# Two-layer encoder on one core: earlier weight requests, a pair normed in the tail, one copy fewer per position half, gathers in another buffer ring

## The chip, the cores and the metric

One core of one Trainium2 chip runs the whole program. TensorE (PE) multiplies, VectorE (DVE) and ScalarE (ACT) work element by element, GpSimd (POOL) does some element-wise work and issues some DMAs, SyncE (SP) issues most DMAs. The metric is the device time of one execution in microseconds (us); the time before is the median of three runs. The stages below come from one further execution that was profiled.

## What is computed

Two sequences (2048 and 512 tokens, width 1024) pass through the same trunk, in fp32:

```python
def trunk(x):
    h = rmsnorm(x, attn_norm)                     # layer 0: windowed attention
    z = h @ attn_w_in                             # q (16 heads x 64), k, v (4 heads), gate
    p = exp(q k^T / 8 + bias[key - query]) over |key - query| <= 128, with a sink in the denominator
    x = x + ((p v) * silu(gate)) @ attn_w_out
    h = rmsnorm(x, fourier_norm)                  # layer 1: Fourier mixing
    f = Re(2-D DFT of h over positions and the 256 channels of each of 4 groups)
    x = x + (f * silu(h @ fourier_w_gate)) @ fourier_w_out
    return rmsnorm(x, final_norm)
```

## The kernel before, in words

Each fp32 operand of a large product is split into a high part (rounded, ACT copy) and a low part (the difference, DVE or POOL), and a product is three matmuls (`matmul3`, L91). Tile pools hand out buffers by tag, each tag a ring of a fixed number of buffers: `x` (`xtile`, 4), `hT` (`htile`, 8), `xr` (3), `w` (4), `uT` (8), and in the second layer `L` (`left`, 20) and `R` (`right`, 16). An instruction that fills a new tile waits until all users of the tile that held the buffer are done. Every engine runs its own queue in order; the order within each queue is planned when the program is built, near the order of the code, with explicit edges added by `after` and `seq` (L127, L132) where one instruction must stand behind another.

**Layer 0** goes through five chunks of 512 tokens (`CHUNKS`, L35; chunk 0 is the short sequence). For a chunk, `make_h` loads the transposed x and splits it, `kv_proj` makes k and v, and a loop of 17 steps (L829) runs the attention of eight head pairs: pair p is scored in steps 2p and 2p+1. In step n `at[n // 2 + 1].start()` (L833) requests the bias tile b of a later pair (L426), and in odd steps `loads[n // 2 + 2]()` (L835) brings the next q and gate weights. In chunk 0 a weight comes raw from DRAM (`load_w`, L96: staging tile w32, L110), is split by ACT (L113) and POOL (L118), and its split form is stored for the later chunks; the staging tile is a `uT` buffer, but for pairs 6 and 7, for two `late` weights and for the output weights it is an `xtile` buffer (L109). The xs tiles, from which the sums of squares of the next chunk are made (`stats`, L150; load L169, square L161), take `xtile` buffers too. The splits of softmax rows (`pts`, L521 on ACT and L522 on DVE) feed the product `av` (L539) with v. What is left of the output projection of the last chunk when its loop ends is the *tail*: two empty steps, eight steps of products for the second half of the columns, and the residual add and store (L620, L621).

**Layer 1** first runs the tail while it splits the gate weights (`take`, L1131) and norms the two x tiles of pair 0 (`norms`, L969: a square on ACT L947, a power on POOL L88, a scaling on DVE L972). Then ten pairs of 128-token tiles go through `gates` (L1070): seven products W, X, Z by a Winograd scheme of 2x2 blocks, with hooks between them that turn the next pair (transposes L980, sums, splits) and make its channel transform z. Gates go to DRAM (s2d, L1087). For each of the positions of the transform, `position` (L1274) multiplies with a table of cosines and sines into an even part a and an odd part b, copies a twice on ACT (L1299 into asb of the `xr` ring, L1303 into the result u), forms the two mirrored results on DVE (L1304, L1305), and multiplies by the gate rows s2 (L1307), which `gated` (L1248) reads on SP, or for a mirrored position gathers by row numbers through POOL (L1256). The output projection follows, first `finish` (L1325), for the last eight positions `Outs` (L1338), where the first product's hook `split_g` (L1619) requests the next position's gate rows, and `reads` (L1605) its go tiles. Places: `xtile` is also the place of the x rows for the residual.

Of the kernel before, what the change touches and what calls it, by code (L numbers as in the profile page):

```python
# [9 lines left out]
F32 = mybir.dt.float32  # L10
# [4 lines left out]
ALU = mybir.AluOpType  # L15
# [4 lines left out]
P = 128  # L20
D = 1024
# [21 lines left out]
def encoder(  # L43
# [52 lines left out]
    def load_w(c, n, name, lo_engine=None, late=None):  # L96
# [12 lines left out]
        w32 = stage[late is not None or n > 19 or n in (6, 7, 18, 19)](f"w32{name}")  # L109
        load = SP.dma_start(w32, w_in[n] if n < 20 else w_out[(n - 20) // 4, (n - 20) % 4])  # L110
        if late:
            after(load, late)
# [12 lines left out]
    stage, res_tile, ready, chain = [], [], {}, {}  # L125
# [15 lines left out]
    def attention_phase():  # L141

        with ExitStack() as es:
# [230 lines left out]
            def qg_proj(c, p, hs, res, invb=None):  # L374
# [3 lines left out]

                def load():
                    st["q"] = load_w(c, p, f"q{c}_{p}", None if p else DVE)  # L380
                    st["g"] = load_w(c, 12 + p, f"g{c}_{p}", None if p else DVE)
# [34 lines left out]
                return load, steps  # L416

            def attention(c, p, res, uTs):
# [5 lines left out]
                def start():  # L424
                    bt = ap.tile([P, 2, 386], F32, tag="bias", bufs=2, name=f"b{c}_{p}")
                    SP.dma_start(  # L426
                        bt[:, :, 1:385],
                        bass.AP(rowd.tensor, rowd.offset + p * 1024, [[1, P], [512, 2], [1, 384]]),
                    )
                    st["bias"] = bt  # L430
# [340 lines left out]
            for c in range(len(CHUNKS)):  # L771
# [15 lines left out]
                loads, work = [], []  # L787
                for p in range(8):
                    load, steps = qg_proj(c, p, hs, res[p], invb0)
                    loads.append(load)  # L790
                    work += steps
# [37 lines left out]
                for n in range(17):  # L829
                    new = (at[n // 2], 2 * (n % 2)) if n < 16 else None  # L830
                    old = (at[(n - 1) // 2], 2 * ((n - 1) % 2)) if n else None
                    if n % 2 == 0 and n < 14:
                        at[n // 2 + 1].start()  # L833
# [64 lines left out]
    def fourier_phase(tail):  # L898
        with ExitStack() as es:
# [170 lines left out]
            def gates(pr, hooks):  # L1070
# [53 lines left out]
                hook(5)  # L1124
                prod(W, A[1, 1], wg["N4"], four, False)
# [36 lines left out]
            pairs[0].x = [ready["x", i] for i in range(2)]  # L1162
            ACT.dma_start(gb, bass.AP(g1.tensor, g1.offset, [[0, P], [1, D]]))
            split_steps = [("T", k) for k in range(4)] + [("B", k) for k in (3, 0, 1, 2)]
            for i, s in enumerate(tail):
                s()
                if i in (3, 5):
                    pairs[0].norms((5 - i) // 2)
                if 1 <= i < 9:
# [57 lines left out]
            for n, pr in enumerate(pairs[:-1]):  # L1227
                nx = pairs[n + 1]
                for i in range(2):
                    nx.load(1 - i)  # L1230
                    nx.norms(1 - i)
# [42 lines left out]
            def position(name, tab, gr, gs, tiles, loads=None, parts=None, between=None):  # L1274
# [4 lines left out]
                asb = main.tile([P, 4, P], F32, tag="xr", bufs=3, name=f"as{name}")  # L1279
                us = [zt(f"u{name}_{i}") for i in range(len(tiles))]  # L1280
                for hf in range(2):
# [16 lines left out]
                    sa = asb[:, 2 * hf : 2 * hf + 2]  # L1298
                    ACT.copy(sa, a[:, :, 0:P])  # L1299
                    for i, u in enumerate(us):  # L1300
# [441 lines left out]
```

## Time and profile before

| | |
|---|---|
| median of 3 runs | 1607.68 us (1607.36 to 1610.32) |
| the profiled execution | 1608.39 us |
| its span, first to last instruction | 1606.6 us |
| mean granted TensorE clock | 0.998 of full speed |
| DMA traffic | 373.88 MB, mean 233 GB/s |
| layer 0, up to the end of the tail's products | about 1077 us |

How to read the profile: a *wait* is idle time of an engine, put down to the instruction that ended it. A timeline row gives start, duration, engine, source line, operation, out<-in, and in brackets the idle time before it with its releaser. A window row gives, for a stretch of the span, its length, the busy time of each engine with the number of instructions, the granted clock, the share of DMA engines that were busy, and GB/s. A group row gives the line, engine, operation, shapes and count, then total busy us, mean ns of one, and idle time before. SPq is the sequencer of SyncE, which issues DMAs. PE spans of matmuls are modelled at their end, so neighbours overlap a little.

### The profile page before, as it was taken

The page shows a single profiled execution, that of the slowest core. Times are in us where ns is not written, and L with a number is a line of the kernel's source. Part 1 is how long each engine was busy: PE and PEld are TensorE (multiplying, and loading weights), DVE is VectorE, ACT ScalarE, POOL GpSimd, SP SyncE. Part 2 cuts the span into 40 slices and gives each one's busy share as a digit, 9 for nine tenths or more (in the row PEclk, how much of TensorE's full clock was granted, in tenths as well). Part 3 has the DMA queues.
Part 4 walks back from the last instruction along what each step waited for, and adds up shares of the span by engine and source line. Part 5 has one row for each costly group of instructions (what it writes and reads, how often), then busy time and mean ns, then how long its engine had stood idle before and what let it go on. Part 6 is the DMA issues. An engine that isn't in the chain of part 4 may idle for free.

```text
span 1606.6 us, 27437 instructions
## 1 busy us (share of the span) xinstructions
PE 1587.6 (99%) x9743; PEld 1320.4 (82%) x9743; DVE 1145.6 (71%) x2785; ACT 881.7 (55%) x2112; POOL 446.0 (28%) x613
## 2 busy tenths in 40 slices
PE   9999999999999999999999999999999999999998
PEld 7887888888888888988788888887888887888876
DVE  6787665777547786377764577658878777889786
ACT  6777634676236684257752476636655554343342
POOL 2466651421404314024222242123112111101100
PEclk9999999999999999999999999999999999999999
DMA  7577695656865567655649556665656569458652
GB/s 295 199 289 278 237 349 213 224 220 210 293 218 204 212 238 252 237 207 214 246 157 334 210 207 221 239 223 197 222 210 237 186 219 402 163 196 306 256 198 92
DMA packets 100579, 373.88 MB, mean 233 GB/s; under 512 B 12139, under 2 KB 22379, under 8 KB 83036
## 3 DMA queue, kind: packets, MB, share of 16 engines
q1 hardware_dynamic: 81708, 297.91, 51.9%
q0 software_dynamic: 16400, 70.04, 11.4%
q10 hardware_dynamic: 2336, 4.20, 0.7%
q8 instruction: 77, 1.26, 0.3%
q14 instruction: 58, 0.48, 0.1%
HBM read 280.84 MB, written 91.26 MB: 232 GB/s over the span
## 4 chain that ended last, share of the span: by engine, by line
PE 84%; DVE 4%; issue 4%; DMA 4%; POOL 2%; ACT 2%; POOLq 0%; SPq 0%; DVEq 0%; ACTq 0%
PE gp L94 13%; PE qp L94 13%; PE op L94 9%; PE spt L94 8%; PE spt L455 6%; PE av L539 6%; PE W L94 5%; PE fo L94 4%; PE vp L94 4%; PE pt L513 3%; PE Wo L94 3%; PE Z L94 2%; DMA w32q<-in_w_in_dram 1%; PE z L94 1%; PE Zo L94 1%
## 5 line engine op out<-in xcount | busy, mean ns | idle before, releaser
L474 DVE CUSTOM_DVE_ANT_0 S<-spt,b 128x385 f32<-128x385 f32 (+1 forms) x315 | 154.1, 527 | 128.4 <-PE spt L455 80.2
L94 PE MATMUL gp<-h,wg 128*128 128x512 f32 x960 | 238.6, 397 | 0.0
L94 PE MATMUL qp<-h,wq 128*128 128x512 f32 x960 | 237.1, 396 | 0.0
L521 ACT CAST pts<-pt 128x384 fp32r<-128x384 f32 (+1 forms) x320 | 123.8, 473 | 176.6 <-PE pt L513 176.5
L94 PEld LDWEIGHTS gp<-h,wg 128*128 128x128 f32 x960 | 175.9, 189 | 43.7 <-issue 9.7
L94 PEld LDWEIGHTS qp<-h,wq 128*128 128x128 f32 x960 | 174.9, 188 | 41.3 <-issue 5.5
L482 ACT ACTIVATE S<-S 128x385 f32<-128x385 f32 (+1 forms) x320 | 190.3, 606 | 20.7 <-DVE S L474 18.0
L522 DVE TENSOR_TENSOR pts<-pt,pts 128x384 fp32r<-128x384 f32 (+1 forms) x320 | 147.5, 522 | 28.3 <-ACT pts L521 28.2
L94 PE MATMUL op<-wo,uT 128*128 128x512 f32 x600 | 140.4, 391 | 0.0
L455 PE MATMUL spt<-kwin,qab 64*128 64x384 f32 (+1 forms) x945 | 132.6, 358 | 0.0
L94 PEld LDWEIGHTS op<-wo,uT 128*128 128x128 f32 x600 | 111.9, 188 | 23.9 <-issue 0.7
L563 POOL TENSOR_TENSOR uT<-o,uT 128x256 fp32r<-128x256 f32 x75 | 55.5, 740 | 249.2 <-ACT uT L562 249.1
L539 PEld LDWEIGHTS av<-pts,v 128*128 128x128 f32 x576 | 101.5, 189 | 22.8 <-ACT pts L521 2.8
L539 PE MATMUL av<-pts,v 128*128 128x512 f32 (+1 forms) x576 | 117.2, 343 | 2.4 <-ACT pts L521 1.8
L94 PE MATMUL fo<-wo,tTu 128*128 128x512 f32 x480 | 116.7, 392 | 0.0
L455 PEld LDWEIGHTS spt<-kwin,qab 64*128 64x128 f32 x945 | 85.9, 185 | 31.2 <-issue 24.7
L94 PEld LDWEIGHTS fo<-wo,tTu 128*128 128x128 f32 x480 | 88.5, 188 | 16.7
L494 DVE TENSOR_SCALAR S<-S 128x384 f32<-128x384 f32 (+1 forms) x192 | 90.4, 471 | 6.4
L559 POOL TENSOR_TENSOR o<-o,s 128x256 f32<-128x256 f32 x75 | 55.2, 736 | 134.7 <-DVE o L557 134.4
L94 PE MATMUL spt<-wo,uT 128*128 128x512 f32 x360 | 86.7, 392 | 0.0
L94 PEld LDWEIGHTS spt<-wo,uT 128*128 128x128 f32 x360 | 66.5, 188 | 13.7
L513 PEld LDWEIGHTS pt<-ident,S 64*128 64x128 f32 x1792 | 68.2, 138 | 4.2 <-issue 2.3
(317 smaller groups left out, 3039.4 us busy)
## 6 DMA issues: line engine op xcount, KB each, us to landing
wo<-wsd SPq DMA_DIRECT2D x32, 1024.0 KB, 6.0
wq<-wsd SPq DMA_DIRECT2D x31, 1024.0 KB, 7.4
wg<-wsd SPq DMA_DIRECT2D x31, 1024.0 KB, 5.0
x<-x1d SPq DMA_DIRECT2D x40, 512.0 KB, 4.1
b<-b21d SPq DMA_DIRECT2D x40, 512.0 KB, 5.8
b<-rowd SPq DMA_DIRECT2D x40, 384.0 KB, 4.3
xs<-in_x_dram SPq DMA_DIRECT2D x23, 512.0 KB, 6.7
s2d<-gt POOLq DMA_DIRECT2D x40, 256.0 KB, 3.3
```

The costliest lines, as they stand in the source:

```text
L94: pe(PE.matmul(out, a[i], b[j], start=start and i + j == 0, stop=stop and i == 1, skip_group_check=more))
L455: pe(PE.matmul(banks[j][:, 2 + k0 * P : 2 + k1 * P], res["q"][rows, qp, b * P : (b + 1) * P], kwin[g][rows, kp, b * P + k0 * P : b * P + k ...
L474: seq(DVE, DVE.tensor_tensor_reduce(out=s[:, e0:e1], in0=ps[:, 1 + e0 : 1 + e1], in1=st["bias"][:, j, 386 - e1 : 386 - e0][:, ::-1], scale ...
L482: last_exp[0] = seq(ACT, ACT.activation(s[:, e0:e1], s[:, e0:e1], AF.Exp, bias=s[:, 386:387], scale=-1.0, accum_out=s[:, 387:388]))
L494: seq(DVE, DVE.tensor_scalar(s[:, ks], s[:, ks], den, None, ALU.mult))
L513: pe(PE.transpose(ps[h][:, kb, j, :], ss[j][rows, 1 + kb * P : 1 + (kb + 1) * P], ident[rows, rows]))
L521: seq(ACT, ACT.copy(hi, ps[:, k0:k1]))
L522: seq(DVE, DVE.tensor_tensor(lo, ps[:, k0:k1], f32(hi), ALU.subtract))
L539: pe(PE.matmul(to, v, pt, start=n == part == 0, stop=part == 1 and n in (1, len(todo) - 1), skip_group_check=n > 1,))
L559: eng.tensor_tensor(o, o, s, ALU.mult)
L563: low = eng.tensor_tensor(lo, o, f32(hi), ALU.subtract)
```

## The change

Five edits in one:

1. `fetch_w` is split off `load_w`. In chunk 0 the raw weights of pairs 6 and 7 are requested at the start of steps 8 and 10 (before: in steps 9 and 11), and the bias request of that step is put behind them.
2. The x tiles of pair 1 of the Fourier layer are loaded in the tail (after steps 4 and 5, into `htile` buffers) and normed there (after steps 8 and 10), no longer at the start of pair 0's gates.
3. For the last pair of `gates`, hook 5 stands in the middle of the N4 product instead of ahead of it.
4. `position` copies a once, into the first result; the second result takes only its two edge columns from ACT, and DVE forms all else from the first result, whose real part is overwritten last.
5. `split_g` puts the second tile of gate rows, the gathered one, into `left` always; before it was `xtile` in all but the first round.

```diff
--- before.py
+++ after.py
@@ -93,7 +93,16 @@
         for i, j in ((0, 0), (0, 1), (1, 0)):
             pe(PE.matmul(out, a[i], b[j], start=start and i + j == 0, stop=stop and i == 1, skip_group_check=more))
 
-    def load_w(c, n, name, lo_engine=None, late=None):
+    def fetch_w(n, name, late=None):
+
+        w32 = stage[late is not None or n > 19 or n in (6, 7, 18, 19)](f"w32{name}")
+        load = SP.dma_start(w32, w_in[n] if n < 20 else w_out[(n - 20) // 4, (n - 20) % 4])
+        if late:
+            after(load, late)
+        last_fetch[0] = load
+        return w32
+
+    def load_w(c, n, name, lo_engine=None, late=None, w32=None):
 
         w = wp.tile([P, 2, D], F32R, align_bytes=LINE, tag="w", bufs=4, name=f"w{name}")
         if c == 1 and n in AGAIN:
@@ -106,10 +115,8 @@
         if c:
             SP.dma_start(f32(w), f32(wsd[n]))
             return w[:, 0], w[:, 1]
-        w32 = stage[late is not None or n > 19 or n in (6, 7, 18, 19)](f"w32{name}")
-        load = SP.dma_start(w32, w_in[n] if n < 20 else w_out[(n - 20) // 4, (n - 20) % 4])
-        if late:
-            after(load, late)
+        if w32 is None:
+            w32 = fetch_w(n, name, late)
         ACT.copy(w[:, 0], w32)
         if lo_engine is None:
 
@@ -122,7 +129,7 @@
             (SP if lo_engine else POOL).dma_start(f32(wsd[n]), f32(w))
         return w[:, 0], w[:, 1]
 
-    stage, res_tile, ready, chain = [], [], {}, {}
+    stage, res_tile, ready, chain, last_fetch = [], [], {}, {}, [None]
 
     def after(ins, anchor):
 
@@ -376,9 +383,13 @@
                 steps = []
                 st = {}
 
+                def fetch():
+                    for which, n in (("q", p), ("g", 12 + p)):
+                        st["w32" + which] = fetch_w(n, f"{which}{c}_{p}")
+
                 def load():
-                    st["q"] = load_w(c, p, f"q{c}_{p}", None if p else DVE)
-                    st["g"] = load_w(c, 12 + p, f"g{c}_{p}", None if p else DVE)
+                    for which, n in (("q", p), ("g", 12 + p)):
+                        st[which] = load_w(c, n, f"{which}{c}_{p}", None if p else DVE, w32=st.get("w32" + which))
 
                 def mm(which, k):
                     if k == 0:
@@ -413,7 +424,7 @@
 
                 for which, evac in (("q", evac_q), ("g", evac_g)):
                     steps += [lambda which=which, evac=evac, k=k: one(which, evac, k) for k in range(KD)]
-                return load, steps
+                return fetch, load, steps
 
             def attention(c, p, res, uTs):
 
@@ -421,12 +432,13 @@
                 g = p // 2
                 st = {}
 
-                def start():
+                def start(behind=None):
                     bt = ap.tile([P, 2, 386], F32, tag="bias", bufs=2, name=f"b{c}_{p}")
-                    SP.dma_start(
+                    load = SP.dma_start(
                         bt[:, :, 1:385],
                         bass.AP(rowd.tensor, rowd.offset + p * 1024, [[1, P], [512, 2], [1, 384]]),
                     )
+                    after(load, behind)
                     st["bias"] = bt
                     uT = wp.tile([P, 2, CH], F32R, align_bytes=LINE, tag="uT", bufs=8, name=f"uT{c}_{p}")
                     uTs.append((uT[:, 0], uT[:, 1]))
@@ -784,9 +796,10 @@
                 uTs = []
                 res = [{} for p in range(8)]
                 at = [Heads(*attention(c, p, res[p], uTs)) for p in range(8)]
-                loads, work = [], []
+                fetches, loads, work = [], [], []
                 for p in range(8):
-                    load, steps = qg_proj(c, p, hs, res[p], invb0)
+                    fetch, load, steps = qg_proj(c, p, hs, res[p], invb0)
+                    fetches.append(fetch)
                     loads.append(load)
                     work += steps
                 loads[0]()
@@ -829,8 +842,13 @@
                 for n in range(17):
                     new = (at[n // 2], 2 * (n % 2)) if n < 16 else None
                     old = (at[(n - 1) // 2], 2 * ((n - 1) % 2)) if n else None
+                    behind = None
+                    if c == 0 and n in (8, 10):
+
+                        fetches[n // 2 + 2]()
+                        behind = last_fetch[0]
                     if n % 2 == 0 and n < 14:
-                        at[n // 2 + 1].start()
+                        at[n // 2 + 1].start(behind)
                     if n % 2 and n // 2 + 2 < 8:
                         loads[n // 2 + 2]()
                     chain.setdefault(PE, None)
@@ -1121,8 +1139,12 @@
                 x_step(3)
                 DVE.tensor_tensor(c11, c11, X, ALU.add)
                 silu(c11, 0, 0)
-                hook(5)
-                prod(W, A[1, 1], wg["N4"], four, False)
+                if pr is not pairs[-1]:
+                    hook(5)
+                prod(W, A[1, 1], wg["N4"], (0, 1), False)
+                if pr is pairs[-1]:
+                    hook(5)
+                prod(W, A[1, 1], wg["N4"], (2, 3), False)
                 silu(W, 1, 0)
                 hook(6)
 
@@ -1160,12 +1182,22 @@
             order = [[16, 17, 18, 19]] + [[a, a + 4, a + 8, a + 12] for a in range(4)]
             pairs = [Pair(2 * gi + i // 2, tiles[i : i + 2]) for gi, tiles in enumerate(order) for i in (0, 2)]
             pairs[0].x = [ready["x", i] for i in range(2)]
+
+            def second(i):
+
+                t = pairs[1].x[i] = htile([P, D], F32, f"x1_{pairs[1].ts[i]}")
+                SP.dma_start(t, x1d[pairs[1].ts[i] * P : (pairs[1].ts[i] + 1) * P, :])
+
             ACT.dma_start(gb, bass.AP(g1.tensor, g1.offset, [[0, P], [1, D]]))
             split_steps = [("T", k) for k in range(4)] + [("B", k) for k in (3, 0, 1, 2)]
             for i, s in enumerate(tail):
                 s()
                 if i in (3, 5):
                     pairs[0].norms((5 - i) // 2)
+                if i in (4, 5):
+                    second((4, 5).index(i) ^ 1)
+                if i in (8, 10):
+                    pairs[1].norms((8, 10).index(i) ^ 1)
                 if 1 <= i < 9:
                     w, k = split_steps[i - 1]
                     take(ready[w, k], k, left, *{"T": ("T2", "T1"), "B": ("B11", "B22")}[w])
@@ -1226,9 +1258,10 @@
                 build(k)
             for n, pr in enumerate(pairs[:-1]):
                 nx = pairs[n + 1]
-                for i in range(2):
-                    nx.load(1 - i)
-                    nx.norms(1 - i)
+                if n:
+                    for i in range(2):
+                        nx.load(1 - i)
+                        nx.norms(1 - i)
                 gates(pr, {
                     1: [lambda: turns1(nx)], 2: [lambda: turns2(nx)], 3: [lambda: turns3(nx)], 4: [lambda: turns4(nx)],
                     5: [lambda: nx.z_odd_even()],
@@ -1276,7 +1309,6 @@
                 s2s, tb = loads or position_loads(name, tab, tiles)
                 cs, sn, ns = [(tb[:, 2 * i], tb[:, 2 * i + 1]) for i in range(3)]
                 bp = bank(f"B{name}")
-                asb = main.tile([P, 4, P], F32, tag="xr", bufs=3, name=f"as{name}")
                 us = [zt(f"u{name}_{i}") for i in range(len(tiles))]
                 for hf in range(2):
                     ts = parts[hf] if parts else halves_of(name, gr, gs, hf)
@@ -1295,14 +1327,15 @@
                     acc(a, (cs, ns), 0, 130)
                     b = bp[:, hf * 256 : hf * 256 + 256].rearrange("p (g c) -> p g c", g=2)
                     acc(b, (sn, cs), P, P)
-                    sa = asb[:, 2 * hf : 2 * hf + 2]
-                    ACT.copy(sa, a[:, :, 0:P])
-                    for i, u in enumerate(us):
-                        uv = u.rearrange("p (g c) -> p g c", g=4)[:, 2 * hf : 2 * hf + 2]
-                        ops = (ALU.subtract, ALU.add) if i == 0 else (ALU.add, ALU.subtract)
-                        ACT.copy(uv[:, :, 0 : P + 1], a[:, :, 0 : P + 1])
-                        DVE.tensor_tensor(uv[:, :, 1:P], sa[:, :, 1:P], b[:, :, 1:P], ops[0])
-                        DVE.tensor_tensor(uv[:, :, P + 1 : 256], sa[:, :, 1:P], b[:, :, 1:P], ops[1])
+                    uv = [u.rearrange("p (g c) -> p g c", g=4)[:, 2 * hf : 2 * hf + 2] for u in us]
+                    ACT.copy(uv[0][:, :, 0 : P + 1], a[:, :, 0 : P + 1])
+                    re, im = uv[0][:, :, 1:P], b[:, :, 1:P]
+                    for v in uv[1:]:
+                        ACT.copy(v[:, :, 0 : P + 1 : P], a[:, :, 0 : P + 1 : P])
+                        DVE.tensor_tensor(v[:, :, 1:P], re, im, ALU.add)
+                        DVE.tensor_tensor(v[:, :, P + 1 : 256], re, im, ALU.subtract)
+                    DVE.tensor_tensor(uv[0][:, :, P + 1 : 256], re, im, ALU.add)
+                    DVE.tensor_tensor(re, re, im, ALU.subtract)
                 for u, s2 in zip(us, s2s):
                     DVE.tensor_tensor(u, u, s2, ALU.mult)
                 return list(zip(us, tiles))
@@ -1618,8 +1651,7 @@
 
                 def split_g():
 
-                    places = (xtile, xtile if ft["N4"] else left)
-                    nxt["s"] = [gated(name, r, place) for r, place in zip(tiles, places)]
+                    nxt["s"] = [gated(name, r, place) for r, place in zip(tiles, (xtile, left))]
                     nxt["p"] = [halves_of(name, *gl, hf) for hf in range(2)]
                     if not ft["T3"]:
                         f_sums("T3", right)
```

## The prediction

> **What bounds the kernel now.** I read the page first, then who TensorE waited for, then the stages around the longest waits, cut with the window view.
>
> ```profile
> span 1606.6 us, 27437 instructions
> PE 1587.6 (99%) x9743; PEld 1320.4 (82%) x9743; DVE 1145.6 (71%) x2785; ACT 881.7 (55%) x2112; POOL 446.0 (28%) x613
> ...
> PE av L539 <- ACT pts L521: 1.8, 1, 1.8
> PE tr L1350 <- DVE up L1307: 1.6, 2, 0.8
> ...
> PE trb L980 <- DVE x L972: 1.0, 1, 1.0
> PE W L94 <- ACT c L1097: 1.0, 1, 1.0
> ```
>
> TensorE is busy for 1587.6 of 1606.6 us, and the change removes no matmul. So what can be won is the 19.0 us of its idle time, and whatever slower clock follows an idle stretch. The longest waits lie in four places, and each edit touches one. The sum below is made against the profiled execution: 1608.39 us, 1.79 us more than its span, and 0.71 above the median 1607.68.
>
> **Part 1, weights of pairs 6 and 7 (chunk 0).** The windows below are steps 9, 11 and 13 of the 17-step loop (columns: us; busy us of PE, PEld, DVE, ACT, POOL; clock; DMA share; GB/s), then two cuts of step 11.
>
> ```profile
> 117.43:126.70 9.27, 9.09 (x64) 7.09 (x63) 6.30 (x25) 7.96 (x20) 7.01 (x11) 1.00 0.38 133
> 135.60:148.44 12.84, 10.99 (x65) 8.28 (x64) 8.49 (x29) 9.49 (x22) 8.23 (x12) 0.87 0.60 223
> 148.44:157.23 8.79, 8.79 (x63) 7.10 (x62) 7.45 (x26) 6.50 (x18) 7.58 (x11) 1.00 1.00 376
> ...
> 140.00:142.38 2.38, 0.63 (x3) 0.19 (x1) 1.24 (x4) 2.38 (x6) 2.35 (x4) 1.00 0.02 9
> ...
> 144.20:146.20 2.00, 2.00 (x7) 1.61 (x7) 1.88 (x11) 2.00 (x6) 2.00 (x4) 0.50 0.87 252
> ```
>
> Steps 9 and 11 split the weights of pairs 6 and 7. A step without a stall takes 8.79 us; step 9 took 9.27 and step 11 took 12.84, so 0.48 and 4.05 us too much. Only 1.8 us of that is idle TensorE; the rest is the clock, 0.50 in the two microseconds after it. The chain behind it, from the timeline, with one line of the chain of work (DMA w32q, 12.41 us to landing):
>
> ```profile
> 119.81 2.84 POOL L118 TENSOR_TENSOR wq<-w32q,wq 128x256 fp32r<-128x256 f32 x4 [1.48 <-ACT wq L113]
> ...
> 123.54 0.38 SPq L426 DMA_DIRECT2D b<-rowd  x1
> 124.01 1.80 SPq L169 DMA_DIRECT2D xs<-in_x_dram  x2
> 126.42 0.33 SPq L110 DMA_DIRECT2D w32q<-in_w_in_dram  x1
> ...
> 126.42 12.41 DMA w32q<-in_w_in_dram
> ...
> 138.91 1.05 ACT L113 CAST wq<-w32q 128x1024 fp32r<-128x1024 f32 x1 [3.59 <-DMA w32q<-in_w_in_dram]
> ...
> 144.97 1.04 ACT L161 ACTIVATE xs<-xs 128x1024 f32<-128x1024 f32 x1
> ...
> 147.39 0.19 ACT L437 COPY b<-sk 128x4 f32<-128x4 f32 x1
> ```
>
> SP's queue is in order. Pair 7's q is requested at 126.42, behind bias b (held until its buffer frees) and two xs loads; ACT, free at 138.91 - 3.59 = 135.32, waits for it, and the casts of pts that TensorE's av needs are queued behind on ACT. The edit puts both requests ahead of b. They still need a staging buffer of the xtile ring (4). One that is sure: pair 6's q leaves its buffer when POOL ends, at 119.81 + 2.84 = 122.65. Plus 12.41 that lands at 135.06, just before ACT is free; DMA engines are only 38% busy in step 9, so 12.41 is an upper price. Pair 6 is requested earlier in the same way. I take 4.3 of 0.48 + 4.05 = 4.53; bounds 0 and 4.5. What it costs: b, and the chunk-1 xs loads, come behind two more requests (0.33 us as the q row, g's alike) and their buffers, g's at worst 126.4, so b is 2.9 us later than 123.54; its first user on ACT is at 147.39, some 20 us on. Next late after the stall: nothing near, as step 13 shows, with no idle time at the same ACT load.
>
> [...]
>
> **Part 2, pair 1 of the Fourier layer normed in the tail.** Stage of pair 0's gates, then a later pair's for comparison; then the queues.
>
> ```profile
> 1081.87:1114.98 33.11, 30.44 (x165) 24.80 (x162) 28.40 (x47) 23.99 (x48) 11.20 (x14) 1.00 0.53 190
> ...
> 1140.35:1166.02 25.67, 25.67 (x141) 22.22 (x141) 18.73 (x31) 15.19 (x29) 4.92 (x9) 1.00 0.55 195
> ...
> 1074.98 2.05 DVE L620 TENSOR_TENSOR xr<-xr,op 128x512 f32<-128x512 f32 x3 [4.38 <-PE op L94]
> 1075.96 1.90 POOL L621 DMA_DIRECT2D x1d<-xr  x3 [10.89 <-DVE xr L620]
> ...
> 1077.46 1.07 ACT L987 CAST tTb<-trb 128x512 fp32r<-128x512 f32 x2 [16.72 <-PE trb L980]
> ...
> 1088.25 0.32 SPq L967 DMA_DIRECT2D x<-x1d  x1
> ...
> 1089.85 1.09 ACT L947 ACTIVATE jkb<-x 128x1024 bf16<-128x1024 f32 x1
> ...
> 1092.50 1.76 DVE L972 SCALAR_TENSOR_TENSOR x<-x,invb,g1b 128x1024 f32<-128x1024 f32 x1 [0.74 <-POOL invb L88]
> ```
>
> The first stage takes 7.44 us more. It has 24 more matmuls; at 25.67/141 = 0.18 us each that is 4.4, so 3.0 are waits. Now x is asked for at 1088.25 for want of an xtile buffer, squared on ACT at 1089.85 and scaled on DVE at 1092.50; TensorE waits 1.0 for that and 1.0 for an ACT copy queued among these squares. Moved: per tile one SP load, one square (1.09 on ACT), one one-column power on POOL, a short and a long DVE operation (up to 1.76). Their new cover is the idle time in the last three brackets: 16.72 on ACT, 10.89 on POOL, 4.38 on DVE, for 2.2 us of squares, two powers, and at most 3.8 on DVE. Without that cover the DVE part would stand before the residual adds and cost up to 3.8. On SP the loads pass the last wo loads, which do wait for buffers; a stuck load there would hold them. The x tiles now take two of eight hT buffers, those of split gate weights. Next late is DVE: 28.40 of 33.11 busy, still some 25 of 30. So not all comes back: I take 2.6 of 3.0; bounds -3.8 and 3.0.
>
> **Part 3, hook order and no copy of real parts.** The first row, from the chain of work, is for the time of one product (chunk 1's k).
>
> ```profile
> 221.88 10.88 PE spt L94 x48
> ...
> 1340.02 1.98 PE L932 MATMUL tru<-ident,us 128*128 128x128 f32 x14 [0.50 <-DVE us L1307]
> ...
> 1349.71 0.37 ACT L1299 COPY ass<-As 128x256 f32<-128x256 f32 x1 [1.72 <-DMA s2d<-gt]
> ...
> 1350.41 0.39 PE L94 MATMUL As<-gs,tbs 128*128 128x260 f32 x1 [0.65 <-ACT us L1303]
> ...
> L1303 ACT COPY up<-Ap 128x258 f32<-128x258 f32 x32 | 10.8, 391 | 0.9 <-DVE gp L1270 0.9
> ...
> L1304 DVE TENSOR_TENSOR up<-asp,Bp 128x254 f32<-128x254 f32 x32 | 13.2, 414 | 6.0 <-PE Bp L94 4.5 <-ACT up L1303 1.3
> L1299 ACT COPY asp<-Ap 128x256 f32<-128x256 f32 x18 | 6.7, 374 | 25.0 <-PE Ap L94 15.5 <-DVE gp L1270 9.2
> ```
>
> The transposes at 1340.02 wait 0.50 for DVE; with six N4 products put ahead of them (10.88/48 = 0.23 each, 1.4 us), that wait is covered. The hook's one w_fout load on SP goes 1.4 us later too; I count that at nothing, 1.4 at most. The dropped copy (asb) also held a buffer of the xr ring, and ACT stood 1.72 us at 1349.71 for a gate store that had not landed; that goes, and with it the 0.65 that TensorE waited next. Also gone: 24 copies of 0.37 (18 asp, 6 ass), and 16 of 0.39 shrink to four elements a row, not shown at this place (between 0 and 0.39; 0.19 as the b<-sk row, the nearest). That is 24 x 0.37 + 16 x 0.20 = 12.1 us off ACT, which idles elsewhere there (25.0 us ahead of L1299), so I count it at nothing. DVE keeps its operations (0.41 each); one a half now works in place, which may cost nothing or as much as a second 0.41. I take nothing, since the scaling of x in part 2 works in place too; at 0.41 the two halves that TensorE awaits here lose 0.8. Sum: 0.50 + 0.65 and the small waits right behind them: 1.3; bounds -0.8 and 2.
>
> **Part 4, mirrored gathers in the left ring.**
>
> ```profile
> 1502.06:1527.04 24.98, 24.13 (x126) 20.20 (x125) 21.15 (x37) 10.61 (x22) 3.25 (x5) 1.00 0.53 194
> 1527.04:1553.26 26.22, 24.99 (x126) 20.31 (x124) 22.55 (x40) 12.26 (x25) 2.47 (x3) 1.00 0.60 204
> 1553.26:1577.21 23.95, 23.95 (x125) 20.41 (x124) 21.29 (x37) 11.25 (x23) 2.45 (x3) 1.00 0.48 164
> ...
> 1518.65 1.01 POOL L1256 DMA_INDIRECT s2p<-s2d,mir  x1 [4.73 <-DVE up L1305]
> ...
> 1543.32 1.01 POOL L1256 DMA_INDIRECT s2p<-s2d,mir  x1 [4.79 <-DMA out_dram<-x]
> ```
>
> Three rounds of the same products take 24.98, 26.22 and 23.95 us: 1.03 + 2.27 = 3.3 over the last. In the first two the gather is issued late, waiting for an xtile buffer (in the second, for an output store to land), and TensorE then waits 1.6 for DVE's product with it. In left, 16 of 20 buffers hold w_out and N4; four are free for F (two), a table and this tile, so it need not wait. The xtile buffer it leaves lets the x loads on SP go earlier, and the go loads behind them. I take 2.3; bounds 0 and 3.3.
>
> **Sum.** 4.3 + 2.6 + 1.3 + 2.3 = 10.5: 1608.39 - 10.5 = 1597.9; against the median 1597.2. I forecast **1597.5**. By their upper bounds the parts give 12.8 to 14 together with the small waits near them: 1594.
>
> **Rivals.**
>
> ```profile
> 221.96 1.28 DVE L211 SCALAR_TENSOR_TENSOR h<-xk,g0s,h 128x512 fp32r<-128x512 f32 x1 [3.87 <-ACT h L210]
> ```
>
> - *Pair 7 is still late*: the ring gives its buffer only at about 126.4. Part 1 shrinks to 0.5: 1601.7. For it: four buffers for four weights and five xs tiles. Against: 122.65 is enough.
> - *Given back in chunk 1*: its h tiles come from a DMA and POOL chain that does not move. Against: the seventh h is done at 221.96 + 1.28 = 223.24 and wanted at 221.88 + 6/8 x 10.88 = 230.0 (its products are the row of 48), 6.8 us later. If so, 1608.39 - 6.2 = 1602.2.
> - *DVE takes over in the Fourier layer* (86% busy in pair 0's stage and in the slow round): only part 1 comes, 1604.1.
> - *Idle time alone comes back*: the clock falls for another reason; part 1 gives 1.8 + 0.5, so 1599.9. [...]
> - *Not what it says*: the order that is planned at compile time keeps the requests and norms where they were: 1607.7.
> - *Slower*: pair 7's request gets the buffer of the last xs tile, whose square ends at 144.97 + 1.04 = 146.0. With 12.41 it lands at 158.4, 19.6 us after 138.83; ACT, and so TensorE, stand that much longer: 1608.4 - 6.2 + 19.6 = 1622. It passes the old time once the request goes out later than 126.4 + 6.2 = 132.6. Against: two buffers come free before.
>
> **How the numbers follow.** Forecast 0.50; pair 7 still late 0.15; chunk 1 0.05; DVE 0.13; idle alone 0.04; nothing 0.05; slower 0.08. A measurement tells 0.2% (3.2 us) from no change, so faster is below 1604.5, slower above 1610.9. Faster: 0.50 + 0.15 + 0.05 + 0.04 and half of the DVE case, 0.80; within: its other half and nothing, 0.12; slower 0.08. The range, 1593.5 to 1604.5, takes in all but the last two and half of the DVE case.
>
> **What would show it.** Part 1: w32q for pair 7 issued before b and by 123, no ACT wait at its cast, step 11 near 8.8 with clock 1.00. Part 2: pair 1's squares before the transposes of pair 0; the stage near 30.5. Part 3: no wait ahead of tru and As. Part 4: gathers about 10 us earlier, rounds near 24. I am wrong if step 11 still shows a wait for w32q, if b is late, or if new DVE waits of a microsecond stand in the Fourier stages.

## The result and the profile after

| | before | after |
|---|---|---|
| median, beside each other on one chip | 1607.52 us (6 runs, 1605.77 to 1610.32) | 1595.33 us (6 runs, 1594.02 to 1596.69) |
| the profiled execution | 1608.39 us | 1594.57 us |
| TensorE idle | 19.0 us | 11.2 us |

The ratio is 0.9924, with a 95% interval from 0.9911 to 0.9936: 12.2 us faster by the medians, 13.8 by the two profiled executions. Forecast were 1597.5 us, and 10.5 us off. Line numbers behind L95 are higher in the kernel after: the product av is now at L551, ACT's casts of pts at L533, the add to c at L1136, the gather at L1289.

First the page after, span and busy time, then all that TensorE waited for over 0.2 us (total, times, longest).

```profile
span 1592.8 us, 27377 instructions
...
PE 1581.6 (99%) x9743; PEld 1319.4 (83%) x9743; DVE 1145.4 (72%) x2785; ACT 871.7 (55%) x2088; POOL 447.5 (28%) x613
```

```profile
PE idle L239 <- DVE idle L236: 1.2, 1, 1.2
PE W L94 <- DVE c L1136: 1.0, 1, 1.0
PE Bp L94 <- DVE up L1338: 0.3, 1, 0.3
PE Ap L94 <- DVE gp L1303: 0.3, 1, 0.3
```

Every wait that the prediction quoted from before is gone, and one of 1.0 us is new (W for DVE's c). Of the 13.8 us, 7.8 are idle time; the other 6.0 are a shorter busy time of the same 9743 matmuls. Now the stages, cut at the same matmuls as before: steps 9, 11 and 12 of chunk 0, pair 0's stage, and two of the last rounds. (The prediction calls its third window step 13; it begins where step 11 ends, so it is step 12.)

```profile
117.29:126.11 8.82, 8.82 (x64) 7.16 (x63) 7.59 (x28) 8.14 (x22) 2.54 (x4) 1.00 0.99 377
...
134.22:143.08 8.86, 8.86 (x65) 7.21 (x64) 7.83 (x29) 8.17 (x21) 6.04 (x9) 1.00 0.69 226
143.08:151.86 8.78, 8.78 (x63) 7.09 (x62) 7.83 (x27) 6.89 (x18) 6.40 (x10) 1.00 0.89 318
...
1070.38:1107.68 37.30, 36.81 (x212) 31.43 (x211) 31.05 (x51) 25.90 (x52) 11.26 (x16) 1.00 0.56 206
1508.26:1532.22 23.96, 23.96 (x125) 20.32 (x124) 21.15 (x37) 10.07 (x21) 4.06 (x4) 1.00 0.60 192
1532.22:1556.16 23.94, 23.94 (x126) 20.32 (x124) 21.17 (x37) 10.16 (x21) 3.45 (x3) 1.00 0.59 193
```

Read the first two numbers of a row: where they agree, TensorE never stood. Step 9 is 8.82 (9.27 before), step 11 is 8.86 (12.84), at clock 1.00. Pair 0's stage, here cut from its first transpose to the next pair's first Z, is 37.30 us long (1076.83 to 1117.27 before: 40.44). The rounds are even at 23.95.

The whole difference, by the starts of the same matmuls in the two profiles:

| from | to | before | after | gained |
|---|---|---|---|---|
| start | first product of chunk 1 | 221.71 | 216.30 | 5.41 |
| there | first transpose of pair 0 | 855.12 | 854.08 | 1.04 |
| there | first Z of pair 1 | 40.44 | 37.30 | 3.14 |
| there | last X of the last pair | 221.41 | 220.52 | 0.89 |
| there | transposes of the second position | 48.96 | 47.72 | 1.24 |
| there | first Xo | 107.15 | 107.58 | -0.43 |
| there | last Xo | 96.04 | 93.50 | 2.54 |

The rows add up to 13.83. The 1.04 belongs to no part: item 4 alone, whose code there is that of before, takes 853.94 for the same stretch. The last row differs between executions too: seven profiles have the rounds of before, and take 96.04 to 97.91 us from first to last Xo; that of the kernel before is the shortest of them.

### The profile page after: what moved, and what is told of

It reads as the page before. It is cut to its first block, busy times and chain, and to the rows that moved or that the text cites. A ratio compares the mean times of both kernels' runs of the same rounds, so it can differ in the third digit from the quotient of the medians.

```text
span 1592.8 us, 27377 instructions
## 1 busy us (share of the span) xinstructions
PE 1581.6 (99%) x9743; PEld 1319.4 (83%) x9743; DVE 1145.4 (72%) x2785; ACT 871.7 (55%) x2088; POOL 447.5 (28%) x613
## 5 line engine op out<-in xcount | busy, mean ns | idle before, releaser
L533 ACT CAST pts<-pt 128x384 fp32r<-128x384 f32 (+1 forms) x320 | 123.5, 473 | 176.2 <-PE pt L525 176.1
L551 PEld LDWEIGHTS av<-pts,v 128*128 128x128 f32 x576 | 101.4, 188 | 18.7
L551 PE MATMUL av<-pts,v 128*128 128x512 f32 (+1 forms) x576 | 115.7, 341 | 0.0
```

What stands on the lines that cost most here:

```text
L533: seq(ACT, ACT.copy(hi, ps[:, k0:k1]))
L551: pe(PE.matmul(to, v, pt, start=n == part == 0, stop=part == 1 and n in (1, len(todo) - 1), skip_group_check=n > 1,))
```

## The experiments

Twelve kernels. Each median stands beside runs of the kernel before on the same chip (its median in brackets). To begin with, each part alone on the kernel before.

### The parts alone

Part 1 (diff item 1) alone:

> The kernel before with the early weight requests alone. Theory (each part removes its own wait, and the parts add): step 11 falls from 12.84 to about 8.9 us and steps 9 and 10 by 0.5 together to 1.3, so 5.2 us less by the two profiles, 1602.4; the Fourier stages stay as before, with the waits of 1.0 for x and for c in pair 0's gates. Rival (what the chunk loop wins, a later DMA-bound stage takes back): step 11 is short, but chunk 1 or the tail begins less than 3 us earlier, 1605 or more. Rival (the clock falls for another reason than the wait): the clock of 0.5 stays somewhere in steps 9 to 13, 1605.

Measured: 1602.56 us (1608.11), ratio 0.9965 [0.9953, 0.9978], 5.55 us off.

Part 2 (item 2) alone:

> The kernel before with pair 1's load and norm in the tail alone. Theory: pair 0's gate stage gets 3 to 4 us shorter, because ACT and DVE lose two squares and two scalings there, 1604.0; nothing else changes. Rival (it only moves the wait: DVE is 86% busy in that stage and the next one): the waits for x and c go, others of the same total come, less than 1.5 us, 1606.5. Rival (the tail pays): TensorE idles between the tail's last product and the first transposes by more than a microsecond.

Measured: 1604.6 us (1608.11), ratio 0.9977 [0.9968, 0.9987], 3.5 us off. Pair 0's stage is 37.19 us.

Of part 3, item 4 alone, so without the hook edit:

> The kernel before without the copy of real parts, with the hook where it was. Theory (the gain of part 3 is the copy's alone, since in the changed kernel a wait of 1.0 for DVE's add of c stands where the hook's wait of 0.5 was): the wait of 0.65 ahead of the As products goes, together with ACT's 1.72 for the gate store, and the wait of 0.5 for the turned tile stays: 1.3 to 1.6 us less, 1606.2. Rival (the hook's move gave it): less than 0.5 us, 1607.2.

Measured: 1606.35 us (1608.11), ratio 0.9989 [0.998, 0.9999], 1.8 us off. TensorE's timeline after the last X of the last pair is that of the kernel after, though the hook stands where it stood before:

```profile
1336.71 0.84 PE L94 MATMUL X<-b,tTb 128*128 128x512 f32 x3
1338.57 1.69 PE L94 MATMUL W<-wN,tTb 128*128 128x512 f32 x6 [1.01 <-DVE c L1118]
1340.09 1.04 PE L932 MATMUL tru<-ident,us 128*128 128x128 f32 x8
```

Six N4 products (W<-wN) now run ahead of the transposes (tru), and they wait 1.01 us, where the theory kept the wait of 0.50 for the turned tile.

Part 4 (item 5) alone:

> The kernel before with the gathered gate rows in the left ring alone. Theory: the second and third gather are issued some 10 us earlier, the two waits of 0.8 for DVE's product with them go, the rounds come to about 24 us: 2.5 us less, 1605.2. Rival (the gain came from the ACT copies that part 3 removes in the same rounds): the gathers are early, but the rounds keep more than half of the 3.3 us, 1606.5.

Measured: 1605.03 us (1608.11), ratio 0.9981 [0.9971, 0.999], 3.1 us off.

The four add up to 13.9 us, and together they give 12.2: nothing shows that one part takes much from another.

**What the same code shows five times.** Layer 0 is the same in the kernels before, part 2 alone, item 4 alone, part 4 alone and the load of part 2 alone (below). Still its step 11 waited 1.75, 1.16, 1.66, 0.51 and 0.46 us, and steps 9 to 12 took 39.80, 38.63, 38.55, 37.26 and 37.35 us, against 34.57 after. So part 1 is worth 5.2, 4.1, 4.0, 2.7 or 2.8 us by these steps, according to the execution; the profile on which the prediction rests held the largest. The wait goes with one transfer: pair 7's q, requested 9.2 us ahead of step 11 each time, took 12.4, 11.8, 12.3, 11.1 and 11.1 us to land.

### Which of the two requests?

Part 1 alone with the early request of only one pair:

```diff
-                    if c == 0 and n in (8, 10):
+                    if c == 0 and n == 8:
```

> The kernel before, with the early request for pair 6 alone (at step 8); pair 7's weights are asked for as before, behind bias b and the xs tiles. My theory: the stall of step 11 is pair 7's q, requested at 126.4 and 12.4 us on its way. Then only step 9's 0.5 us comes back, step 11 still waits 0.5 to 1.8 us for the casts of pts, and the time is 1607.3 (1606.5 to 1608). Rival, the delay begins with pair 6 and is handed on (pair 6's late split holds the staging buffers of pair 7): most of part 1 comes, 1604 or less, and step 11 is near 8.9 us.

Measured: 1603.26 us (1607.12), ratio 0.9978 [0.9968, 0.9987], 3.9 us off. Its steps 9 and 11, and SP's queue between them:

```profile
117.01:125.83 8.82, 8.82 (x63) 7.16 (x62) 7.59 (x28) 7.46 (x21) 2.54 (x4) 1.00 0.67 223
...
133.94:142.80 8.86, 8.86 (x63) 7.21 (x63) 8.18 (x28) 8.54 (x22) 7.43 (x12) 1.00 0.50 139
```

```profile
121.23 0.38 SPq L437 DMA_DIRECT2D b<-rowd  x1
121.77 0.84 SPq L176 DMA_DIRECT2D xs<-in_x_dram  x2
122.71 0.38 SPq L99 DMA_DIRECT2D w32q<-in_w_in_dram  x1
```

The rival holds: step 11's stall is gone, although pair 7's q is still asked for behind b and two xs tiles. With pair 6 in time, b's buffer is free at 121.23 instead of 123.54, and all behind it comes earlier: q at 122.71 instead of 126.42. It also lands in 6.8 us instead of 12.4; the DMA engines are 60% busy in step 10, 97% before, but that this is the reason is not shown.

The other way round, `n == 10`:

> The kernel before, with the early request for pair 7 alone (at step 10). My theory: step 11's stall goes, step 9 keeps its 0.5 us: about 1603.1, 5.0 us off where part 1 whole gives 5.5, with step 11 near 8.9 us and no wait for the casts of pts. Rival, pair 6 late keeps its staging buffer until 122.7, so that pair 7's request goes out no earlier than 123 although it stands ahead of b: step 11 still waits 0.3 to 1 us and the time is 1605 to 1607.

Measured: 1605.01 us (1607.12), ratio 0.9986 [0.9976, 0.9995], 2.1 us off. Steps 9 and 11, then the requests:

```profile
117.03:126.49 9.46, 9.29 (x65) 7.09 (x64) 6.32 (x25) 7.99 (x20) 7.04 (x11) 1.00 0.50 175
...
135.37:144.23 8.86, 8.86 (x63) 7.17 (x62) 7.72 (x29) 8.07 (x21) 6.03 (x8) 1.00 0.88 319
```

```profile
122.44 0.33 SPq L99 DMA_DIRECT2D w32q<-in_w_in_dram  x1
...
126.59 0.41 SPq L437 DMA_DIRECT2D b<-rowd  x1
```

Step 11 has no stall here either, with q requested at 122.44 and landed 4.0 us later. The trace is the theory's, but the time is not: 1603.1 was expected, and its 5.0 us off lie outside the interval (0.8 to 3.9). So the stall has two ways out, and either is enough; what only pair 6's request gives is 0.6 us in step 9 and 0.8 in step 10. Pair 7 alone comes out 1.8 us behind pair 6 alone, which fits these 1.4 though the two intervals overlap.

### Without the order edge

Part 1 alone, with both requests made early but no edge that puts b behind them:

```diff
-                        at[n // 2 + 1].start(behind)
+                        at[n // 2 + 1].start()
```

> Part 1 whole, but without the rule that bias b comes behind the requests: the planner then puts b ahead of them on SP, in both steps, though the requests are made two steps early. My theory: SP's queue is in order and b stands until its buffer is free (104.6 and 123.5), so that the requests go out at about 106 and 125, as before; nothing comes back but a little: 1607 (1605.5 to 1608). Rival, it is enough that the requests stand ahead of the xs tiles, which wait for buffers of the same ring: pair 7 goes out by 124, lands by 136, and 4 us or more come back: 1604 or less.

Measured: 1613.48 us (1607.12), ratio 1.0037 [1.0022, 1.0051]: 6.4 us slower than before, which neither theory had. Steps 9 and 10 (8.82 and 8.11 us after), then ACT's queue and TensorE's waits:

```profile
117.27:131.57 14.30, 10.77 (x65) 8.47 (x64) 10.42 (x35) 12.63 (x31) 9.53 (x14) 0.88 0.48 171
131.57:145.02 13.45, 10.15 (x60) 7.57 (x59) 7.21 (x26) 8.26 (x20) 4.19 (x7) 0.87 0.74 270
```

```profile
111.28 0.53 ACT L494 ACTIVATE S<-S 128x257 f32<-128x257 f32 x1
...
117.18 1.05 ACT L120 CAST wq<-w32q 128x1024 fp32r<-128x1024 f32 x1 [5.28 <-DMA w32q<-in_w_in_dram]
118.13 0.61 ACT L494 ACTIVATE S<-S 128x385 f32<-128x385 f32 x1
```

```profile
119.89 0.34 PE L525 MATMUL pt<-ident,S 64*128 64x64 f32 x4 [1.72 <-ACT S L504]
121.16 0.27 PE L525 MATMUL pt<-ident,S 64*128 64x64 f32 x1 [0.93 <-DVE s L414]
122.31 0.83 PE L525 MATMUL pt<-ident,S 64*128 64x64 f32 x11 [0.88 <-ACT xs L168]
...
138.88 0.50 PE L551 MATMUL av<-pts,v 128*128 128x512 f32 x1 [3.02 <-ACT pts L533]
```

As I expected, SP's queue stood at b: the requests went out at 105.91 and 127.05, hardly other than before (107.00 and 126.42). What I had not counted is ACT. In step 9 its cast of q now stands ahead of three activations of S and the xs square, which before ran ahead of it. So ACT stands 5.28 us, and 6.37 at the next cast, with the softmax rows that TensorE wants queued behind. Why the cast moved was not tried; the order is planned at build time, and I take it that the plan counts from the early request. A request moved in the code but held in the queue was worse than a late one.

### The hook of part 3

The kernel after with the hook of the last pair back in its old place (item 3 undone):

> The kernel after, with the hook of the last pair back in its old place (all transposes of us asked for ahead of the N4 products). Theory, formed from the run of the copy edit alone: the planner orders TensorE by readiness and puts six N4 products ahead of the transposes in either case, so the hook edit does nothing: 1595.3, as after, within 1 us, with the same 1.0 us wait of the first N4 product for DVE. Rival, the step as I predicted it (the hook edit covers 0.5 us): 1595.8 to 1596.3, with a wait ahead of the transposes.

Measured: 1595.01 us (1607.12), ratio 0.9927 [0.991, 0.9943]. TensorE's work there stands in the order of the kernel after, with the same wait:

```profile
1327.73 0.84 PE L94 MATMUL X<-b,tTb 128*128 128x512 f32 x3
1329.57 1.65 PE L94 MATMUL W<-wN,tTb 128*128 128x512 f32 x6 [1.00 <-DVE c L1136]
```

The hook edit does nothing that these runs can show.

### The copy of real parts, back in the kernel after

The run of item 4 alone was mixed with the unsteady stall of layer 0. So it was undone (the `-` and `+` lines of `position` exchanged) in the kernel after, where that stall is gone:

> The kernel after without the edit of the real parts: the copies into their own tile are back (one on ACT per half, DVE's sums from the copy), the hook edit and parts 1, 2 and 4 stay. In the run of the copy edit alone the gain, 1.8 us with an interval from 0.2 to 3.2, was mixed with a wait in the layer before that differs from run to run; here that wait is gone. Theory, part 3 as predicted: 1.3 us are lost, 1596.6 (1596.0 to 1597.3), the waits of the transposes for DVE (0.5) and of As for ACT (0.65) are back although the hook edit is in. Rival: the copy edit only moves waits (0.85 us won before the transposes, 0.5 lost in the rounds behind them): 1595.3 to 1595.8.

Measured: 1596.53 us (1608.68), ratio 0.9922 [0.9909, 0.9936]. Against its own neighbours it is as good as after, and 1.2 us above after's median; 1.2 us is below what these ratios tell apart. The traces say more. TensorE and ACT of this run:

```profile
1330.55 1.98 PE L950 MATMUL tru<-ident,us 128*128 128x128 f32 x14 [0.50 <-DVE us L1340]
...
1340.92 0.39 PE L94 MATMUL As<-gs,tbs 128*128 128x260 f32 x1 [0.62 <-ACT us L1336]
```

```profile
1340.21 0.37 ACT L1332 COPY ass<-As 128x256 f32<-128x256 f32 x1 [1.70 <-DMA s2d<-gt]
```

With the copies back and the hook edit still in, the transposes are ahead of the N4 products again, and both waits of the prediction, 0.50 and 0.65, are back (the second, ahead of the even part As, is 0.62 here), with ACT's 1.70 for the gate store. From the last X to the transposes of the second position this run takes 48.94 us, before 48.96, after 47.72. From there to the first Xo it is the other way: 107.13 here, 107.15 before, 107.58 after. Between first and last Xo, 94.12 here and 93.50 after; the run without the hook edit, whose rounds are those of after, takes 93.93.

### The buffers of part 4

The kernel after, with the two tiles of a round exchanged:

```diff
-                    nxt["s"] = [gated(name, r, place) for r, place in zip(tiles, (xtile, left))]
+                    nxt["s"] = [gated(name, r, place) for r, place in zip(tiles, (left, xtile))]
```

> The kernel after, with the two tiles of a round exchanged: the one that SP reads takes the left buffer, the mirrored gather an xtile buffer. Theory, as predicted: the gather's wait for an xtile buffer was the cost, so it is late again in at least one round and 2 to 3 us are lost: 1597.5 to 1598.5, with a wait of TensorE for DVE's product with the gathered tile. Rival: what helped is that a round takes one xtile buffer fewer, whichever tile leaves; then 1595.3 as after, within 1 us, rounds near 24 us.

Measured: 1594.17 us (1607.36), ratio 0.9917 [0.9902, 0.9932]: as after. The gathers and the Xo products of two rounds:

```profile
1495.61 1.27 POOL L1289 DMA_INDIRECT s2p<-s2d,mir  x1 [5.72 <-DVE F L1407]
1522.92 1.01 POOL L1289 DMA_INDIRECT s2p<-s2d,mir  x1 [4.76 <-DVE x L1431]
```

```profile
1508.08 2.88 PE L94 MATMUL Xo<-wo,tT 128*128 128x512 f32 x12
1531.98 2.88 PE L94 MATMUL Xo<-wo,tT 128*128 128x512 f32 x12
```

The gather still waits for an xtile buffer, 4.76 us here as 4.73 and 4.79 before, and it costs nothing: it is issued 9.1 us ahead of its round's Xo (1522.92 and 1531.98), where before it came 0.1 us ahead (1518.65 and 1518.74). With one user fewer in the ring, the wait ends earlier. The rival holds: which tile leaves the ring does not matter.

### The load of part 2

Part 2 alone, with the loads in the tail and the norms back behind pair 0's steps in the code:

```diff
-                if i in (8, 10):
-                    pairs[1].norms((8, 10).index(i) ^ 1)
...
-                if n:
-                    for i in range(2):
-                        nx.load(1 - i)
-                        nx.norms(1 - i)
+                for i in range(2):
+                    if n:
+                        nx.load(1 - i)
+                    nx.norms(1 - i)
```

> The kernel before, with pair 1's loads moved into the tail and its norms left behind pair 0's steps. Theory, as predicted: both count; the load removes the wait of trb for DVE's x (1.0 us), but the squares still stand ahead of the copy of c on ACT, so the 1.0 us wait of W for ACT stays: 1605.5 to 1606.5. Rival: the late load is the whole cause and the norms are planned to wherever their data are: 1604.6, as part 2 alone, with neither wait.

Measured: 1603.24 us (1607.36), ratio 0.9975 [0.9966, 0.9984], 4.1 us off. ACT's squares of pair 1's x:

```profile
1057.75 1.05 ACT L947 ACTIVATE jkb<-x 128x1024 bf16<-128x1024 f32 x1
...
1062.60 1.06 ACT L947 ACTIVATE jkb<-x 128x1024 bf16<-128x1024 f32 x1 [3.71 <-DMA x<-x1d]
```

They run in the tail, before the first transpose at 1073.93, though the code has them behind pair 0's steps. Both waits of TensorE are gone, and the stage is 37.39 us (37.19 with the norms moved by hand). The rival holds: the load is the whole edit, and the planner brings the norms along.

### The new wait

The kernel after, with the product of u and gate rows made half by half:

```diff
                     DVE.tensor_tensor(re, re, im, ALU.subtract)
-                for u, s2 in zip(us, s2s):
-                    DVE.tensor_tensor(u, u, s2, ALU.mult)
+                    h = slice(512 * hf, 512 * hf + 512)
+                    for u, s2 in zip(us, s2s):
+                        DVE.tensor_tensor(u[:, h], u[:, h], s2[:, h], ALU.mult)
```

> The kernel after, with DVE's product of u with the gate (1.22 us for a whole tile) done half by half, each as soon as that half of u is there. Theory: the 1.0 us wait of the first N4 product is DVE's queue, in which a whole product stands ahead of the add that frees W; the first halves fit into DVE's idle 1.2 us ahead of it, so the wait falls to 0.4 us or less, and the small waits of the later rounds with it: 1594.3 (1593.5 to 1595). Rival: the halves cost more on DVE (two starts instead of one, some 0.1 us for each of 18 tiles) and the gates are wanted earlier than they land: 1595.3 to 1597, with new waits for the gate's DMA on DVE.

Measured: 1594.59 us (1607.36), ratio 0.9918 [0.9905, 0.9932], which can't be told from after. For the halves, the kernel after shows 1.22 us for such a product of 1024 columns and 0.685 for DVE's add to c of 512, so some 0.15 more for two halves, as an estimate. The 1.0 us wait is gone, and others took its place:

```profile
PE Ap L94 <- DVE gp L1303: 0.9, 1, 0.9
PE fo L94 <- ACT tTu L956: 0.7, 1, 0.7
```

So no version was found that beats the kernel after by more than can be measured.

## Why the prediction was right, point by point

**Part 1: right in size and in its first way, but the cause was only half of it.** Predicted 4.3 of at most 4.5; the medians of part 1 alone give 5.55 (3.5 to 7.6 by the interval of its ratio), steps 9 to 12 give 5.2 against the profile before and 2.7 to 4.1 against the other four. The 5.2 passes the bound because of step 10 (8.90 us before, 8.11 after), for which the prediction had no term. SP's queue of the kernel after:

```profile
90.82 0.54 SPq L99 DMA_DIRECT2D w32q<-in_w_in_dram  x1
...
104.43 0.38 SPq L437 DMA_DIRECT2D b<-rowd  x1
...
116.83 0.33 SPq L99 DMA_DIRECT2D w32q<-in_w_in_dram  x1
...
121.47 0.38 SPq L437 DMA_DIRECT2D b<-rowd  x1
```

Pair 7's q goes out at 116.83, ahead of b and before 123, as forecast; "pair 7 is still late" did not come. The step "it lands at 135.06, just before ACT is free" is right in its conclusion, and pair 7's request alone shows that it is enough, but not in its figure: the transfer, priced at 12.41 us, took 7.4 in the kernel after, whose cast starts at 125.32 without a wait. But pair 6's, which I gave 0.48 us, removes the same stall alone, because b's buffer and the queue behind it come free earlier. Bias b was priced as late by up to 2.9 us; it is 2.1 earlier (121.47 for 123.54). *Given back in chunk 1* did not come: the 5.41 us of its start stay won. That 4.3 was near is in part luck: it was sized on the largest of five stalls and left out step 10.

**Idle time alone, the clock.** It was a rival. Steps 9 to 12 of the profile before have 39.80 us with TensorE busy for 37.37, so 2.43 idle; after, they take 34.57 and no idle time: 5.2 came back, and the clock of step 11 went from 0.87 to 1.00. So more than idle time came back. Part of it does even without the clock: item 4 alone has 38.55 us there, 2.58 of them idle, at clock 1.00 throughout, and is 4.0 us over the kernel after. Of its other 1.4 us, 0.49 lie in the product av behind the wait (six matmuls in 1.79 us, 1.30 after), and 0.36 and 0.45 in the busy time of steps 10 and 12. So the reading that all but 1.8 us of step 11's excess "is the clock" was too simple: a clock of 0.87 over 12.84 us loses, as I estimate, 0.13 x 12.84 = 1.7 of the 4.05. The wait here was 1.75 us, and a clock of 0.50 followed it, from 143.50 to 146.92. But in the four other executions of this code the clock stayed at 1.00 (below), so the 0.50 is not part of every run.

**Part 2: right, but for what it takes.** Predicted 2.6 of at most 3.0; pair 0's stage is 3.1 us shorter, and part 2 alone took 3.5 off (2.1 to 5.1 by its interval). The predicted 30.5 us for the stage are 37.8 in the cut used here, and 37.30 were measured. Both 1.0 us waits are gone. In part 4 alone and pair 7 alone these two waits were followed by a clock of 0.50, and the stage took 41.65 and 41.67 us instead of 40.44, so in some executions the part is worth 1.2 us more. *DVE takes over* did not come: 31.05 of 37.30 us busy, with no wait over 0.3 us. The cost of DVE work without cover, up to 3.8, did not show. What I took for two moved things is one: the load.

**Part 3: right in sum, wrong in cause.** Predicted 1.3 = 0.50 + 0.65 and little else. The step "with six N4 products put ahead of them, that wait is covered" names the wrong edit: the hook edit changes nothing that can be seen (I take it that the order is planned by what is ready); item 4 changed the order. Nor is the wait covered; a wait of 1.01 for DVE's c stands in its place. The prediction named new DVE waits of a microsecond in the Fourier stages as a sign that it is wrong, and for this step the sign is right: that the sum came out is luck. The step on the asb buffer is right: ACT's 1.7 us for the gate store comes and goes with it, and with it TensorE's 0.65. By the traces, against the kernel with the copies: 1.2 won up to the transposes, 0.45 lost after them, 0.2 to 0.6 won in the last rounds, so 1.0 to 1.4; the times can't tell it from nothing. The small copy, priced at 0.19 us, took 0.169, and the operation in place 0.413, the same as out of place:

```profile
L1334 ACT COPY up<-Ap 128x4 f32<-128x4 f32 x14 | 2.4, 169 | 2.8 <-DVE gp L1303 2.8
...
L1338 DVE TENSOR_TENSOR up<-up,Bp 128x254 f32<-128x254 f32 x18 | 7.3, 413 | 0.0
```

**Part 4: right in size, wrong in mechanism.** Predicted 2.3; first to last Xo went from 96.04 to 93.50 us, 2.5 less, and part 4 alone took off 3.1; against the longest of the seven profiles with the old rounds it is 4.4. The step "it need not wait" is true of the kernel after, but it isn't what counts: the swapped kernel's gathers do wait. What counts is one xtile user fewer per round.

**Not what it says** proved true of one edit, the hook, and of the norms' place. **Slower** did not come, but the run without the order edge shows that the side was real: by another mechanism than mine, ACT's planned order instead of a late ring buffer, and for 6.4 us instead of 14.

**The sum.** 10.5 predicted, 12.2 measured, and 13.8 by the profiles. Part 1's 5.4 for 4.3 is the largest miss of a term; part 2 is 0.5 over, part 3 and part 4 together (1.24 - 0.43 + 2.54 = 3.35 for 3.6) are near. The other 1.9 lie in two stretches for which the prediction had no term: 1.04 that differs between executions of the same code, and 0.89 behind pair 0's stage, of which part 2 alone shows 0.25 (221.16 us) and its load alone all (220.51, after 220.52). So the load can bring it; why the two differ is open.

## What to carry to other kernels

A late transfer in an in-order queue can have its cause a round earlier (pair 7's q went out at 126.42 us, and at 122.71 with pair 6 in time): before moving a request, ask which earlier lateness holds the buffer in front of it, and try each request alone. If a planner orders the queues, move the load, whose place it keeps to, and check in the trace where the consumers landed; a request that only seems earlier can pull its consumers forward and cost more than it saves (6.4 us slower here). A wait for a ring buffer may be cured by taking any user out of the ring (1595.33 us with the gathered tile out, 1594.17 with the other). And profile the same code more than once before a stall is priced: here one stall was 0.46 us in one execution and 1.75 in another.

## What the runs showed of the hardware

**The clock.** After a short stall it was not the same each time. In the kernel before, a wait of 1.75 us, ended at 142.38, was followed by a granted clock of 0.50; in item 4 alone, 1.66 us in the same place, ended at 142.45, were not, nor were 1.16, 0.51 and 0.46 us (part 2, part 4 and the load of part 2 alone). The kernel before, then item 4 alone:

```profile
140.00:142.38 2.38, 0.63 (x3) 0.19 (x1) 1.24 (x4) 2.38 (x6) 2.35 (x4) 1.00 0.02 9
...
143.50:146.92 3.42, 3.42 (x10) 2.73 (x10) 3.21 (x15) 3.40 (x11) 3.10 (x6) 0.50 0.84 256
146.92:148.44 1.52, 1.52 (x9) 0.94 (x7) 1.23 (x3) 1.52 (x3) 1.23 (x2) 1.00 0.99 407
```

```profile
142.45:144.45 2.00, 1.91 (x8) 1.41 (x9) 1.97 (x10) 2.00 (x8) 1.68 (x3) 1.00 0.24 39
144.45:146.45 2.00, 2.00 (x11) 1.65 (x10) 1.89 (x9) 2.00 (x6) 2.00 (x4) 1.00 0.80 256
```

In the kernel without the order edge, three waits of 1.72, 0.93 and 0.88 us, ended between 119.89 and 122.31, were followed by 0.50, and so was one of 3.02, ended at 138.88:

```profile
122.85:124.85 2.00, 2.00 (x15) 1.58 (x12) 1.61 (x6) 1.98 (x6) 2.00 (x4) 0.50 1.08 446
...
140.00:142.00 2.00, 2.00 (x7) 1.61 (x7) 1.97 (x11) 1.82 (x5) 0.85 (x2) 0.50 0.42 27
```

So were two waits of 1.0 us, some 2.2 us apart, in pair 0's stage of part 4 alone and of pair 7 alone; in the kernel before the same two were not (clock 1.00 over the whole 40.44 us). Part 4 alone:

```profile
1091.92:1095.34 3.42, 3.42 (x13) 3.00 (x12) 2.69 (x4) 1.84 (x4) 1.50 (x3) 0.50 1.04 412
```

So the length of the wait alone does not tell: near 1.7 us it was followed by 0.50 in one execution and not in another, and the two of 1.0 us were in two executions and not in a third. A stall can cost the clock in one execution and not in the next; what decides it was not shown.

Why the transfer of pair 7's q takes 11.1 us in one execution and 12.4 in another was not settled.
